# A hybrid encoder layer on one core: the order of feed-forward pairs, and buffers for copies of memory keys and values

## The chip, the core and the metric

The kernel runs on one core of one Trainium2 chip. A core has five engines that work side by side, each with a queue of its own that it serves in order: TensorE (matrix products; PE in the profile, and PEld for its weight loads), VectorE (DVE), ScalarE (ACT), GpSimd (POOL) and SyncE (SP), which here issues the DMA transfers between the device's memory (HBM) and the memory on the core (SBUF, 128 partitions wide). Products are gathered in PSUM, eight banks of 128 x 512 float32, which DVE and ACT read. The metric is the device time of one execution in microseconds (us), the median of several runs.

## The reference

One layer of an encoder for 1024 tokens of width 1024: a mixer (windowed attention beside a gated delta rule), a cross-attention into 256 memory tokens, and a feed-forward block, each between two RMS norms. What matters here is the memory's keys and values and the feed-forward block:

```python
def _memory_cross_attention(h, mem_n, w_q, w_kv, w_o):
    ...
    kv = mem_n @ w_kv
    k = kv[..., :D_MODEL].reshape(b, m, CROSS_HEADS, CROSS_HEAD_DIM).astype(jnp.float32)
    v = kv[..., D_MODEL:].reshape(b, m, CROSS_HEADS, CROSS_HEAD_DIM).astype(jnp.float32)
    ...

def _swiglu(h, w_gate_up, w_down):
    gu = h @ w_gate_up
    return (jax.nn.silu(gu[..., :D_FF]) * gu[..., D_FF:]) @ w_down
```

All inputs are float32; `D_FF` is 2816, and `w_gate_up` has 1024 rows and 2 x 2816 columns, the gate's columns first.

## The kernel before

Every large product is made of three: a float32 operand is split into a rounded part `hi` (a cast on ACT) and the rest `lo` (a subtraction on DVE, or on POOL where the code says so), and hi x hi, hi x lo and lo x hi are summed in PSUM. `load_w` and `pair_weights` load a raw weight block (`wraw`, two buffers in all) and split it.

The program is written with a framework that schedules: it takes the operations in the order of the code, with the priorities that the code sets for weight loads, models when each could run, and fixes from that one order for each engine. At run time each engine keeps to that order, and waits where an operand isn't ready. A buffer that is used again waits for the last readers of what it held, transfers out of it among them.

**Memory keys and values** (L883 to L912). They are computed while the mixer's scan runs, in slots of a hand-written order (`ORDER_3`): eight times `K`, keys for 128 columns, and then two times `V`, values for 512 columns and both halves of the memory tokens. Each result is copied by ACT from PSUM into a buffer (`cv`, 128 x 256, two buffers; `vv`, 128 x 512, one buffer) and stored to HBM from there. The last windows of the attention (`ptw`, `pow`, L598 to L666) are worked off among the `V`s, and behind them begins the output projection `mid_gemm` (`pmg`, L991), whose PSUM banks are those of the scan, the keys and the values.

**Feed forward, gate and up** (L1155 to L1306). The hidden width of 2816 is 22 blocks of 128 channels, taken in 11 pairs. For each pair, the gate's 256 columns and the up part's 256 columns are each one "weight" of 2 x 2 blocks, multiplied with the activations, 2 x 2 blocks as well, by Strassen's scheme in Winograd's form, with seven block products instead of eight. A block product (`product`, L1163) is 4 k-tiles x 3 parts = 12 matmuls of 128 x 512. In the code the products of one weight are

- A: the first block with X11, and later a second one with X21 added into the same bank;
- B: S2 with T2;
- D: S1 with T1, and later S4 with X22 added into the same bank;
- E: S3 with T3, and later W22 with T4 added into the same bank.

S1 to S4 are sums of weight blocks: POOL makes two of them from the raw blocks `a_` and `b_` (L1215, L1217) and DVE two (L1216, L1218); each is split (`s0h`/`s0l` to `s3h`/`s3l`: S1 is number 0, S2 number 1, S3 number 2, S4 number 3). W22, the lower half of `b_`, is split into `bhi` and `blo`. Between products DVE forms v = A + B (L1279) and u = v + D (L1281), and then the four quarters of the result (`quarter`): for the gate a sum on DVE and SiLU on ACT, for the up part a sum on DVE (`up`, L1242) and on POOL the product with the gate's quarter (L1243). v and u are read out of B's and D's banks before the second product into D may begin.

For the first EARLY = 4 pairs the two products into A are made before this loop, while the last activations are still being prepared (L1173 to L1190); they are kept in HBM (`d_m1`, and the finished quarter in `d_a["11"]`) and fetched in the loop (L1266, L1272). So an early pair has 10 products in the loop, a full one 14. A full pair also needs the whole first block `a_` split (`whi` on ACT, `wlo` on POOL, L1225); an early one doesn't.

For each pair the loop runs over its two weights twice: first A (if full), B, D, E of the gate and then of the up part, and then the second products. After the last quarter come four sums on DVE (`s1`, `s2`, `a21`, `s4`, L1297 to L1301); these and the quarters are stored to `d_a` for the down projection, by `put` behind the loads of the pair after (L1262). Down projection and final norm follow in `block_product` (L1334 to L1460). Index `kb` of the stores is the pair's number, so the order of the pairs makes no difference to what is computed.

Of the kernel before, what the change touches and what calls it, by code (L numbers as in the profile page):

```python
# [10 lines left out]
F32 = mybir.dt.float32  # L11
# [8 lines left out]
P = 128  # L20
# [9 lines left out]
ML = 256  # L30

EARLY = 4
# [43 lines left out]
def tile_hybrid_block(  # L76
# [31 lines left out]
    def pool(name, bufs, **kw):  # L108
        return tc.tile_pool(name=name, bufs=bufs, reuse_waits="tile", **kw)
# [8 lines left out]
    def load_w(src, k, n, eng=None, after=None):  # L118

        with tc.high_priority(AHEAD):  # L120
            raw = wp.tile([P, k, n], F32, tag="wraw", name="wraw")
            with ExitStack() as order_:
                if after:
                    order_.enter_context(tc.issue_after(after.ins))
                nc.sync.dma_start(raw, src.rearrange("(k p) n -> p k n", p=P))
            hi = wp.tile([P, k, n], F32R, tag="whi", name="whi")
            lo = wp.tile([P, k, n], F32R, tag="wlo", name="wlo")
            split(hi, lo, raw, eng=eng)
        return hi, lo
# [726 lines left out]
    mk = p2.enter_context(pool("mk", 1))  # L856
# [26 lines left out]
    def next_keys():  # L883

        ct = kv_done[0]
        kv_done[0] += 1
        whi, wlo = load_w(w_ckv[:, ct * P:(ct + 1) * P], KT, P, nc.gpsimd)
        pp = pc.tile([P, 512], F32, tag="pc", name="pck")[:, 0:ML]
        for k in range(KT):
            for i, (w, a) in enumerate(((whi, 0), (whi, 1), (wlo, 0))):  # L890
                nc.tensor.matmul(pp, w[:, k, :], mT[a][:, k, :], start=(k == 0 and i == 0), stop=(k == KT - 1 and i == 2))
        cv = mk.tile([P, ML], F32, tag="cv", name="cv", bufs=2)
        nc.scalar.copy(cv, pp)
        nc.sync.dma_start(d_mk[ct * P:(ct + 1) * P, :], cv)

    def next_values():

        ch = kv_done[1]
        kv_done[1] += 1
        pp = [pc.tile([P, 512], F32, tag="pc", name="pcv") for _ in range(2)]  # L900
        for kp in range(4):
            whi, wlo = load_w(w_ckv[kp * 256:(kp + 1) * 256, D + ch * 512:D + (ch + 1) * 512], 2, 512)
            for t in range(2):
                for kk in range(2):
                    k = 2 * kp + kk
                    for i, (w, a) in enumerate(((whi, 0), (whi, 1), (wlo, 0))):
                        nc.tensor.matmul(pp[t], mT[a][:, k, t * P:(t + 1) * P], w[:, kk, :], start=(k == 0 and i == 0),
                                         stop=(k == KT - 1 and i == 2))
        for t in range(2):
            vv = mk.tile([P, 512], F32, tag="vv", name="vv", bufs=1)  # L910
            nc.scalar.copy(vv, pp[t])
            nc.sync.dma_start(d_mv[t, :, ch * 512:(ch + 1) * 512], vv)  # L912

# [2 lines left out]
    def scan_step(pairs):  # L916

        for _ in range(4):
            for s_ in pairs:
                next(s_, None)  # L920

    issue(ORDER_3, {"s": lambda *gs: scan_step([scans[g] for g in gs]), "W": next_windows, "M": memory_norm,
                    "K": next_keys, "V": next_values})
    dump("d_pz", d_pz[0] + d_pz[1])
    dump("d_kv", d_kv)
# [230 lines left out]
    NF = FF // P  # L1156
    NB = NF // 2
# [5 lines left out]
    def product(out_, w, xx, start=True):  # L1163
        for k in range(HK):
            for i, (a, b_) in enumerate(((0, 0), (0, 1), (1, 0))):
                nc.tensor.matmul(out_, w[a][:, k, :], xx[b_][:, k, :], start=(start and k == 0 and i == 0),  # L1166
                                 stop=(k == HK - 1 and i == 2), skip_group_check=not start)
# [5 lines left out]
    for e in range(EARLY):  # L1173
        f = 2 * e
# [23 lines left out]
    def bank(name):  # L1198
        return pg.tile([P, 512], F32, tag="pg", name=name)
# [5 lines left out]
    def pair_weights(c0, early):  # L1205

        with tc.high_priority(AHEAD):
            raws = []
            for i in range(2):
                raws.append(wp.tile([P, KT, P], F32, tag="wraw", name="wraw"))  # L1210
                load = nc.sync.dma_start(raws[i], w_gate_up[:, c0 + i * P:c0 + (i + 1) * P].rearrange("(k p) n -> p k n", p=P))
            a_, b_ = raws
            s = [ws.tile([P, HK, P], F32, tag="sr", name="sr", bufs=3) for _ in range(4)]
            hl = {i: [ws.tile([P, HK, P], F32R, tag=f"s{i}{c}", name=f"s{i}{c}") for c in "hl"] for i in (1, 0, 2, 3)}
            nc.gpsimd.tensor_tensor(s[0], b_[:, 0:HK], b_[:, HK:], ALU.add)  # L1215
            nc.vector.tensor_tensor(s[1], s[0], a_[:, 0:HK], ALU.subtract)  # L1216
            nc.gpsimd.tensor_tensor(s[2], a_[:, 0:HK], b_[:, 0:HK], ALU.subtract)  # L1217
            nc.vector.tensor_tensor(s[3], a_[:, HK:], s[1], ALU.subtract)  # L1218
            for i in (1, 0, 2, 3):
                split(*hl[i], s[i])  # L1220
            W1 = None
            if not early:
                ahi = wp.tile([P, KT, P], F32R, tag="whi", name="whi")
                alo = wp.tile([P, KT, P], F32R, tag="wlo", name="wlo")
                split(ahi, alo, a_, eng=nc.gpsimd)  # L1225
                W1 = (ahi[:, 0:HK], alo[:, 0:HK]), (ahi[:, HK:], alo[:, HK:])
            W22 = [tg.tile([P, HK, P], F32R, tag=n, name=n) for n in ("bhi", "blo")]
            split(*W22, b_[:, HK:])
        return W1, W22, [hl[i] for i in range(4)], load
# [21 lines left out]
    def put(stores, after=None):  # L1251
        for dst, t in stores:
            with ExitStack() as order_:
                if after:
                    order_.enter_context(tc.issue_after(after.ins))
                nc.sync.dma_start(dst, t)

    for f in range(0, NF, 2):
        early = f // 2 < EARLY
        wts = [pair_weights(c0, early) for c0 in (f * P, FF + f * P)]  # L1260

        put(sums, wts[1][3])  # L1262
        act = {(r, hf): tg.tile([P, HALF], F32, tag=f"act{r}{hf}", name=f"act{r}{hf}", bufs=1)
               for r in range(2) for hf in range(2)}
        if early:
            nc.sync.dma_start(act[0, 0], d_a["11"][f // 2])  # L1266
        st = []
        for i, (W1, W22, (S1, S2, S3, S4), _) in enumerate(wts):
            a1, v, u = (tg.tile([P, 512], F32, tag=n, name=n, bufs=b_) for n, b_ in (("a1", 1), ("v", 2), ("u", 1)))
            A = None  # L1270
            if early:
                nc.sync.dma_start(a1, d_m1[f + i])  # L1272
            else:
                A = bank("pA")
                product(A, W1[0], X11)
                nc.scalar.copy(a1, A)
            B_, D_, E_ = (bank(n) for n in ("pB", "pD", "pE"))
            product(B_, S2, T2)
            nc.vector.tensor_tensor(v, a1, B_, ALU.add)  # L1279
            product(D_, S1, T1)  # L1280
            nc.vector.tensor_tensor(u, v, D_, ALU.add)  # L1281
            product(E_, S3, T3)
            quarter(i, act, 1, 1, u, E_)
            st.append((A, D_, E_, v))
        for i, (W1, W22, (S1, S2, S3, S4), _) in enumerate(wts):
            A, D_, E_, v = st[i]
            if A is not None:
                product(A, W1[1], X21, start=False)
                quarter(i, act, 0, 0, None, A)
            product(D_, S4, X22, start=False)  # L1290
            quarter(i, act, 0, 1, v, D_)
            product(E_, W22, T4, start=False)
            quarter(i, act, 1, 0, v, E_)
        kb = f // 2
        a11, a21, a12, a22 = (act[i] for i in ((0, 0), (0, 1), (1, 0), (1, 1)))
        s1, s2 = (tg.tile([P, HALF], F32, tag="sa", name="sa") for _ in range(2))
        nc.vector.tensor_tensor(s1, a21, a22, ALU.add)  # L1297
        nc.vector.tensor_tensor(s2, s1, a11, ALU.subtract)
        nc.vector.tensor_tensor(a21, a11, a21, ALU.subtract)
        s4 = tg.tile([P, HALF], F32, tag="up", name="s4")  # L1300
        nc.vector.tensor_tensor(s4, a12, s2, ALU.subtract)  # L1301
        nc.sync.dma_start(d_a["22"][kb], a22)
        if not early:
            nc.sync.dma_start(d_a["11"][kb], a11)
        sums = [(d_a[n][kb], t) for n, t in (("s1", s1), ("s2", s2), ("s3", a21), ("12", a12), ("s4", s4))]
# [187 lines left out]
```

## Time and profile before

| | us |
|---|---|
| median of 3 runs | 1600.72 (1600.3 to 1604.94) |
| profiled execution, its own time | 1601.45 |
| profiled execution, span from the first to the last instruction | 1599.7 |
| DVE busy over the span | 1034.0 |
| ACT busy over the span | 766.2 |
| POOL busy over the span | 522.8 |
| mean granted TensorE clock | 0.983 of full speed |

The profile is of one execution. Its rows name a line of the code (L1166), an engine, an operation, and the tiles written and read, with buffer numbers left out, and then shape and type; where a row gives a number in brackets, it is the idle time of that engine before the instruction, and what ended it. In the timeline a row begins with its start and length in us. A chain of waits is followed backwards from the last instruction: at each step to what released it. The granted clock is the share of full speed that the clock of TensorE had.

### The profile page before, as it was taken

How to read it: one execution, taken by the hardware profiler on the slowest of the kernel's cores; microseconds unless marked ns; L12 is line 12 of the kernel's file. 1: busy time of each engine (PE TensorE's matmuls, PEld its weight loads, DVE VectorE, ACT ScalarE, POOL GpSimd, SP SyncE). 2: the span in 40 equal slices, each digit the busy share in tenths (PEclk: the TensorE clock that was granted, in tenths of full speed). 3: DMA queues.
4: the chain of work that ended last, by engine and by line, in shares of the span. 5: the costliest groups of instructions: out<-in, count | busy, mean ns of one | idle time of the engine just before them, and what ended most of it. 6: DMA issues, size and time to landing. Idle time of an engine off the chain costs nothing. (4 is left out here: it accounts for less than half of the span.)

```text
span 1599.7 us, 21414 instructions
## 1 busy us (share of the span) xinstructions
PE 1523.6 (95%) x7558; PEld 1274.7 (80%) x7558; DVE 1034.0 (65%) x1596; ACT 766.2 (48%) x1561; POOL 522.8 (33%) x479
## 2 busy tenths in 40 slices
PE   6999889988899989999999999999999999999998
PEld 5877778877799967788888777778888888888786
DVE  6846886967677765454345549778765555587575
ACT  6566543326957785564334566223322323344532
POOL 2367653234335610243301140335433433100021
PEclk9999999998999999999999999999999999999999
DMA  6134258474999675354222254444333333763344
GB/s 205 41 109 124 59 159 239 129 192 122 296 324 277 193 266 191 145 185 152 73 69 80 90 185 139 150 157 152 100 120 118 104 99 99 272 222 108 110 169 160
DMA packets 265400, 247.29 MB, mean 155 GB/s; under 512 B 43960, under 2 KB 200525, under 8 KB 265293
## 3 DMA queue, kind: packets, MB, share of 16 engines
q1 hardware_dynamic: 265293, 245.93, 48.7%
q8 instruction: 59, 0.97, 0.3%
q14 instruction: 48, 0.39, 0.1%
HBM read 175.86 MB, written 67.40 MB: 152 GB/s over the span
## 5 line engine op out<-in xcount | busy, mean ns | idle before, releaser
L102 ACT CAST whi<-wraw 128x1024 fp32r<-128x1024 f32 x108 | 113.3, 1050 | 147.7 <-PE pA L1166 34.5
L103 POOL TENSOR_TENSOR wlo<-wraw,whi 128x1024 fp32r<-128x1024 f32 x48 | 118.4, 2467 | 165.2 <-ACT whi L102 150.8
L260 PE MATMUL pg<-hhi,whi 128*128 128x512 f32 x352 | 141.5, 403 | 0.0
L260 PE MATMUL pg<-hlo,whi 128*128 128x512 f32 x352 | 140.8, 401 | 0.0
L260 PE MATMUL pg<-hhi,wlo 128*128 128x512 f32 x352 | 140.8, 400 | 0.0
L103 DVE TENSOR_TENSOR wlo<-wraw,whi 128x1024 fp32r<-128x1024 f32 x60 | 75.5, 1260 | 86.0 <-ACT whi L102 76.5
L991 PE MATMUL pmg<-whi,b 128*128 128x512 f32 x384 | 120.0, 400 | 2.6 <-ACT whi L102 2.2
L1166 PE MATMUL pA<-s,whi 128*128 128x512 f32 x352 | 109.7, 393 | 1.4 <-ACT m L1183 1.4
L285 DVE SCALAR_TENSOR_TENSOR acc<-cp,cols,acc 128x1024 f32<-128x1024 f32 x48 | 77.8, 1622 | 34.8 <-ACT acc L283 34.1
L991 PEld LDWEIGHTS pmg<-whi,b 128*128 128x128 f32 x384 | 72.3, 191 | 18.2 <-ACT whi L102 2.7
L1243 POOL TENSOR_TENSOR act<-act,up 128x512 f32<-128x512 f32 x33 | 48.2, 1460 | 103.9 <-DVE up L1242 46.1
L260 PEld LDWEIGHTS pg<-hhi,wlo 128*128 128x128 f32 x352 | 67.5, 192 | 13.3
L260 PEld LDWEIGHTS pg<-hhi,whi 128*128 128x128 f32 x352 | 67.6, 192 | 13.2 <-ACT hhi L102 0.3
L260 PEld LDWEIGHTS pg<-hlo,whi 128*128 128x128 f32 x352 | 67.4, 191 | 13.1
L1354 PE MATMUL pdX<-dhl,whi 128*128 128x512 f32 x264 | 76.1, 391 | 1.5 <-DVE zv L1409 0.8
L1166 PEld LDWEIGHTS pA<-s,whi 128*128 128x128 f32 x352 | 65.3, 188 | 15.2 <-ACT m L1183 2.0
L1384 POOL TENSOR_SCALAR frs<-sq 128x1 f32<-128x1 f32 x8 | 11.9, 1497 | 195.8 <-ACT jk L1373 194.9
L1215 POOL TENSOR_TENSOR sr<-wraw 128x512 f32<-128x512 f32 x22 | 29.0, 1318 | 134.1 <-DMA wraw<-in_w_gate_up_dram 120.9
L991 PE MATMUL pmg<-wlo,b 128*128 128x512 f32 x192 | 71.5, 392 | 0.0
L1166 PE MATMUL pA<-s,wlo 128*128 128x512 f32 x176 | 68.8, 392 | 1.6 <-DVE wlo L103 1.6
L102 ACT CAST whi<-araw 128x1024 fp32r<-128x1024 f32 (+1 forms) x36 | 35.4, 982 | 71.3 <-PE pdX L1354 27.6
L103 DVE TENSOR_TENSOR wlo<-araw,whi 128x1024 fp32r<-128x1024 f32 (+1 forms) x36 | 40.8, 1133 | 39.6 <-ACT whi L102 39.4
(411 smaller groups left out, 4272.5 us busy)
## 6 DMA issues: line engine op xcount, KB each, us to landing
wraw<-in_w_gate_up_dram SPq DMA_DIRECT2D x52, 512.0 KB, 4.1
kv<-d_kv SPq DMA_DIRECT2D x32, 512.0 KB, 6.9
wraw<-in_w_in_dram SPq DMA_DIRECT2D x22, 512.0 KB, 4.0
b<-in_w_down_dram SPq DMA_DIRECT2D x20, 512.0 KB, 5.9
araw<-d_as SPq DMA_DIRECT2D x20, 512.0 KB, 3.8
d_kv<-kv SPq DMA_DIRECT2D x8, 1024.0 KB, 6.3
pz<-d_pz SPq DMA_DIRECT2D x32, 256.0 KB, 6.6
wraw<-in_w_ckv_dram SPq DMA_DIRECT2D x16, 512.0 KB, 6.4
```

The lines of the kernel that those rows point to most:

```text
L102: nc.scalar.copy(hi, src)
L103: (eng or nc.vector).tensor_tensor(lo, src, f32(hi), ALU.subtract)
L260: nc.tensor.matmul(p_, w[:, k, :], ah[a][:, k, :], start=(k == 0 and i == 0), stop=(k == nk - 1 and i == 2))
L285: nc.vector.scalar_tensor_tensor(acc, cp[:, t:t + S], taps[t], acc, ALU.mult, ALU.add)
L991: nc.tensor.matmul(pp[t], act[a][:, k, tt], w_[:, kk, :], start=(k == 0 and i == 0), stop=(k == KT - 1 and i == 2))
L1166: nc.tensor.matmul(out_, w[a][:, k, :], xx[b_][:, k, :], start=(start and k == 0 and i == 0), stop=(k == HK - 1 and i == 2), skip_group_ch ...
L1215: nc.gpsimd.tensor_tensor(s[0], b_[:, 0:HK], b_[:, HK:], ALU.add)
L1243: nc.gpsimd.tensor_tensor(o_, o_, up, ALU.mult)
L1354: nc.tensor.matmul(banks[t], a[:, k - k0, tt], w, start=(first and k == 0 and i == 0), stop=(k == NB - 1 and i == 2), skip_group_check=not ...
L1384: nc.gpsimd.tensor_scalar(rs, sq[:, 1, t:t + 1], sq[:, 0, t:t + 1], D * EPS, ALU.add, ALU.add)
```

## The change

There are two edits.

The loop over the pairs no longer takes them from 0 to 10, but an early one (with its first products at hand) and a full one in turn, and then the rest: 0, 4, 1, 5, 2, 6, 3, 7, 8, 9, 10. Each pair does what it did before.

The copies of the memory's keys and values use one tag, `cv`, with two buffers of 512 columns, in place of two buffers of 256 columns for the keys and one of 512 for the values. The keys use the first 256 columns of theirs.

```diff
@@ next_keys
-        cv = mk.tile([P, ML], F32, tag="cv", name="cv", bufs=2)
+        cv = mk.tile([P, 512], F32, tag="cv", name="cv", bufs=2)[:, 0:ML]
         nc.scalar.copy(cv, pp)
         nc.sync.dma_start(d_mk[ct * P:(ct + 1) * P, :], cv)
@@ next_values
         for t in range(2):
-            vv = mk.tile([P, 512], F32, tag="vv", name="vv", bufs=1)
+            vv = mk.tile([P, 512], F32, tag="cv", name="vv", bufs=2)
             nc.scalar.copy(vv, pp[t])
             nc.sync.dma_start(d_mv[t, :, ch * 512:(ch + 1) * 512], vv)
@@ tile_hybrid_block
-    for f in range(0, NF, 2):
+
+    turns = [p for e in range(EARLY) for p in (e, EARLY + e)] + list(range(2 * EARLY, NB))
+    for f in (2 * p for p in turns):
         early = f // 2 < EARLY
         wts = [pair_weights(c0, early) for c0 in (f * P, FF + f * P)]
```

Since the framework fixes the order of each engine from a model of the whole, other instructions move with them. On TensorE the built order differs from that before in two places: among the last attention windows, the values and the first products of the output projection, and in the loop over the pairs. Up to the first and between the two it is the same.

## The prediction

> **What bounds the kernel now.** I read the page first, then the work of each engine by stage, then the chain of waits, and last the timeline of TensorE where the stage rows show idle time.
>
> ```profile
> span 1599.7 us, 21414 instructions
> ...
> PE 1523.6 (95%) x7558; PEld 1274.7 (80%) x7558; DVE 1034.0 (65%) x1596; ACT 766.2 (48%) x1561; POOL 522.8 (33%) x479
> ...
> PE 33%; DMA 1%; DVE 1%; ACT 0%; POOL 0%; issue 0%; SPq 0%; DVEq 0%; POOLq 0%; ACTq 0%
> ```
>
> TensorE is busy for 95% of the span and carries the chain; no other engine is near. So a change can win only in TensorE's idle time or in matmuls that run slowly. The profiled execution took 1601.45 us, 1.75 more than its span, and lies 0.73 above the median of the runs (1600.72); the sums below are made against 1601.45. Both edits sit in stretches that these rows divide (busy time of PE, PEld, DVE, ACT and POOL in each, then the granted clock, the DMA share and GB/s):
>
> ```profile
> 996.07:1379.78 383.71, 378.94 (x1658) 311.76 (x1658) 248.06 (x319) 115.77 (x183) 138.39 (x88) 1.00 0.39 126
> 996.07:1105.00 108.93, 104.16 (x446) 84.17 (x446) 82.81 (x105) 30.97 (x51) 38.84 (x26) 0.98 0.48 152
> 1105.00:1379.78 274.78, 274.78 (x1214) 227.59 (x1213) 165.25 (x215) 84.80 (x132) 99.55 (x62) 1.00 0.35 116
> ```
>
> The first row is the whole loop over pairs, from the first product of pair 0 to the last of pair 10. It has 4 early pairs of 10 products and 7 full pairs of 14: 138 products. One product of 12 matmuls takes 2.72 us in the chain below, so the loop could take 138 x 2.72 = 375.4 us; it takes 383.7. The 8.3 us between are all before 1105: from there TensorE is busy for the whole 274.78 us. Of the 8.3, the idle time is 383.71 - 378.94 = 4.8. The chain of waits (start, length, what) shows the largest piece:
>
> ```profile
> 1039.98 4.87 DMA wraw<-in_w_gate_up_dram
> ...
> 1045.04 1.26 POOL sr L1215
> ...
> 1046.33 1.76 DVE sr L1216
> ...
> 1049.42 0.60 DVE s1l L103
> ...
> 1050.62 0.61 DVE u L1281
> ...
> 1051.36 4.36 PE pD L1166 x12
> 1055.73 2.97 PE pE L1166 x12
> 1058.69 2.72 PE pB L1166 x12
> ```
>
> Read backwards: the second product into pD of pair 1's up weight could not start before `u` was read out of that bank (L1281). On DVE `u` stood behind the preparation of the next weight (pair 2's gate), whose sums waited for POOL's, and these for a load issued at 1039.98. TensorE's timeline has this wait and the other three (idle time in brackets):
>
> ```profile
> 997.82 0.51 PE L1166 MATMUL pB<-b,s1l 128*128 128x512 f32 x1 [1.02 <-DVE s1l L103]
> ...
> 1006.32 0.70 PE L1166 MATMUL pD<-x,s3h 128*128 128x512 f32 x2 [0.46 <-DVE u L1281]
> ...
> 1020.38 0.74 PE L1166 MATMUL pB<-b,s1h 128*128 128x512 f32 x2 [0.21 <-ACT s1h L102]
> ...
> 1029.60 0.39 PE L1166 MATMUL pE<-b,blo 128*128 128x512 f32 x1
> ...
> 1047.96 0.39 PE L1166 MATMUL pE<-b,blo 128*128 128x512 f32 x1
> 1051.36 0.70 PE L1166 MATMUL pD<-x,s3h 128*128 128x512 f32 x2 [3.02 <-DVE u L1281]
> ```
>
> 1.02 + 0.46 + 0.21 + 3.02 = 4.7 us, which is the idle time. After the last one the product at 1051.36 takes 4.36 instead of 2.72 and the next 2.97: 1.64 + 0.25 = 1.9 us more.
>
> Why was the load so late? It needed the buffer of the weight before it, and so the last read of that, `blo` on DVE:
>
> ```profile
> 1035.53 0.69 DVE L1297 TENSOR_TENSOR sa<-act,act 128x512 f32<-128x512 f32 x1 [1.18 <-POOL act L1243]
> ...
> 1039.04 0.68 DVE L103 TENSOR_TENSOR blo<-wraw,bhi 128x512 fp32r<-128x512 f32 x1
> ```
> ```profile
> 1031.99 0.62 ACT L102 CAST bhi<-wraw 128x512 fp32r<-128x512 f32 x1
> ```
>
> Its cast was done on ACT at 1032.6, but `blo` came at 1039.04, since DVE met it behind the sums of pair 0 (L1297 and on), which wait for POOL's products of gate and up, and these for the end of pair 0 on TensorE.
>
> **The feed-forward edit.** It removes and adds no instruction: the pairs run as 0, 4, 1, 5, 2, 6, 3, 7, 8, 9, 10. Loads, splits and stores come in the same number, and SP has the same transfers in another order. What moves is which pair follows which, and with it how much TensorE work covers the chain just read. Call U the end of pair 0's last product on TensorE, 1029.60 + 0.23 = 1029.8. `blo` starts 9.2 after U, the load is issued 10.2 after it, and `u` is done (1050.62 + 0.61) at U + 21.4. Before, TensorE has between U and that `u` 21 matmuls and five products: 4.8 + 13.6 = 18.4. That is 3.0 short, the stall.
>
> In the changed kernel's built order, DVE meets the same things in the same sequence: sums of pair 0, `blo`, preparation of the next pair's gate (now pair 1 behind pair 4), then `u`. TensorE now has 28 matmuls of pair 4's gate (6.3), four products of its up weight (10.9), the three second products of the gate (8.2) and one of the up weight (2.7): 28.1. The chain of 21.4 ends 6.7 us before it is asked for. So 3.02 goes, and with it I take the 1.9 of slow matmuls behind it. Gain: 4.9.
>
> The clock rule has to be weighed here. The page "TensorE: Matmul & The Clock Gate" of the Trainium skill (Part 1: The HAM clock gate) puts the fall to half speed after an idle window of about 3.4 us, and the return after about as much work. The idle time here was 3.02 and half speed followed, so the trace is a little under the rule. If by that rule the slow matmuls were not this stall's, 1.9 less would be gained and the time be about 1596.7.
>
> What full pairs bring with them: per weight a cast on ACT and one split on POOL, and the product A must wait for both. POOL's split is long:
>
> ```profile
> L103 POOL TENSOR_TENSOR wlo<-wraw,whi x8: 2392/2400/2649, 1096.4 to 1223.0; 128x1024 fp32r<-128x1024 f32 x8
> ...
> DMA to landing us min/median/max: 3.6/4.1/6.5
> ```
> ```profile
> 1009.42 0.38 SPq L1211 DMA_DIRECT2D wraw<-in_w_gate_up_dram  x1
> ```
>
> It now stands on POOL ahead of the sums for pair 4's gate, in the tightest place of the loop, where the third weight was already 0.21 late (1020.38). The raw block for it is issued at 1009.42; with 4.1 to land, about 1.1 for the cast and 2.4 for the split it is done at 1017.0, and A can start at 1020.2. The sums are at most 2.4 later than before, and A itself gives them 2.72 of cover. So no stall is added and the 0.21 goes; without that cover it would be 2.4 - 0.2 = 2.2 more. If the load takes its longest 6.5, the split ends at 1019.4: still in time. The first two waits, 1.02 and 0.46, stay, since pair 0 is prepared as before.
>
> Then the meeting of a full pair with the early one behind it. Call V the moment at which the second products of pair 4 begin. In the built order `blo` of pair 1's gate stands on DVE behind the reads of the gate's D and E, which come at V + 8.2; with two reads of 0.6 it starts at V + 9.4. From the issue of a load to the end of `s1l` the chain above took 1049.42 + 0.60 - 1039.98 = 10.0, so pair 1's up weight is ready at V + 19.4. TensorE asks for it after the six second products (16.3) and three first ones of pair 1's gate (8.2), at V + 24.5: 5.1 to spare. This meeting comes three times, after pairs 4, 5 and 6; I take nothing for it, and rival 2 has its price. SP serves its queue in order, and pair 1's second load of `a1` now stands behind the stores of pair 4's sums, some 6 us after V + 16.3 as after U above (1035.53 - 1029.8); what is computed from it must be ready only at the second product into that D, at V + 16.3 + 16.3 + 5.4 = V + 38, so 10 us and more are left. Pairs 7 to 10 run as they do now, without a stall.
>
> Sum for the edit: -3.02 - 1.9 - 0.21 = -5.1.
>
> **The copies of keys and values.** Storage is equal: two buffers of 256 columns and one of 512 before, two of 512 after. The eight copies of keys and four of values, and their stores, stay. What comes is that the first value copies use buffers of the last keys, whose copy ends at 564.9 + 0.4, 18 us before the first value is copied (583.7, the row below it): nothing. What goes is the rule that a value's copy needs the store of the one before it landed:
>
> ```profile
> L893 ACT COPY cv<-pck x8: 350/364/375, 439.8 to 564.9; 128x256 f32<-128x256 f32 x8
> ```
> ```profile
> L911 ACT COPY vv<-pcv x4: 583/590/596, 583.7 to 607.4; 128x512 f32<-128x512 f32 x4
> ...
> DMA to landing us min/median/max: 2.3/2.5/2.8
> ```
> ```profile
> 603.67 0.59 ACT L911 COPY vv<-pcv 128x512 f32<-128x512 f32 x1 [0.55 <-PE pcv L907]
> ...
> 606.87 0.58 ACT L102 CAST ph<-ptw 128x512 fp32r<-128x512 f32 x1
> 607.35 0.60 ACT L911 COPY vv<-pcv 128x512 f32<-128x512 f32 x1
> ```
> ```profile
> 605.82 0.50 PE L661 MATMUL pow<-ph,vhi 128*128 128x512 f32 x1 [0.40 <-ACT ao L665]
> ...
> 607.51 0.50 PE L661 MATMUL pow<-ph,vhi 128*128 128x512 f32 x1 [0.72 <-ACT ph L102]
> 607.84 0.63 PE L991 MATMUL pmg<-whi,s 128*128 128x512 f32 x2
> ...
> 631.74 0.73 PE L991 MATMUL pmg<-whi,s 128*128 128x512 f32 x2 [1.49 <-DVE z L995]
> ```
>
> The last copy was placed at 607.35, 3.1 us behind the end of the third. In the built order the copies now stand in twos, the last ahead of `ao`, so the banks of the output projection (pmg, L991) come free earlier and TensorE gets 20 of its matmuls (4.5 us) before the two reads of attention weights that waited 0.40 and 0.72. I take these 1.1 as gained. The bounds: nothing, if a bank or the weights for pmg come late, or if the 1.49 at 631.74 (it hangs on loads and splits, not on TensorE) grows by what was won; and a loss of one DVE split, 1.26, since splits of the mixer's output now stand ahead of `pl` (L103) there:
>
> ```profile
> L103 DVE TENSOR_TENSOR wlo<-wraw,whi 128x1024 fp32r<-128x1024 f32 x60 | 75.5, 1260 | 86.0 <-ACT whi L102 76.5
> ```
>
> The other wait of the neighbourhood, for weights at 589.06, has its loads in the same place, and so stays with the slow matmuls behind it:
>
> ```profile
> 586.69 0.50 PE L661 MATMUL pow<-ph,vhi 128*128 128x512 f32 x1 [0.90 <-ACT ph L102]
> ...
> 589.06 2.08 PE L907 MATMUL pcv<-whi,mT 128*128 128x512 f32 x4 [1.58 <-ACT whi L102]
> ```
> ```profile
> 590.00:600.00 10.00, 10.00 (x40) 8.20 (x39) 3.79 (x9) 8.29 (x21) 0.93 (x2) 0.74 0.74 246
> ```
>
> 0.90 + 1.58 us are idle, and 0.26 of the 10 us after them, 2.6, is lost to the clock. With the same idle time I leave both; if the slow matmuls did not follow, it would be 2.6 less.
>
> Together: 1601.45 - 5.1 - 1.1 = 1595.2 for a profiled execution, 1594.5 on the scale of the median. I forecast 1594.8.
>
> **Rivals.** (1) The feed-forward gain comes, the one of the copies doesn't (for the reason of the 1.49): 1601.45 - 5.1 = 1596.3, or 1595.6 to 1596.3. The row at 631.74 speaks for it; against it, the loads of the mixer's output are no later in the built order. (2) Slower: the meeting full to early. If the chain from `blo` to `s1l` is longer than its 5.1 of cover, TensorE stalls three times, and each stall of about 3 us drags 1.9 of slow matmuls: 3 x 4.9 - 6.2 = +8.5, so 1610. It decides from a chain of over 15.1 us instead of 10.0; two loads at their longest (6.5 against 4.1) add 2.4, POOL's split ahead of a sum another 2.4, which makes 14.8. That is close below, which keeps it alive. (3) The change does nothing that shows: the order moves the 3 us stall to another place in the loop, as the start of pair 4 (2.2 plus 1.9 slow) would; 1601.45 - 6.2 + 4.1 = 1599.3.
>
> Beside (3) stands a rule that speaks against the edit: "GPSIMD Engine Reference" of the Trainium skill (section 1, Specifications) says that POOL shares its way to SBUF with VectorE when that reads two SBUF inputs. The 1.76 of the DVE sum at 1046.33, beside 0.60 for its neighbours, agrees. By it each of the six splits of pairs 4 to 6 slows a DVE operation by up to 1.76 - 0.60 = 1.2 us; each place has 2.7 to 6.7 of cover, so the sum stays.
>
> **Numbers.** Forecast 0.50; (1) 0.17; (2) 0.14; (3) 0.19. The measurement can tell about 0.3%, 4.8 us: faster is below 1595.9, slower above 1605.5. The forecast lies 1.1 below that border, so I give 0.45 of its 0.50 to faster, and of (1), which straddles it, 0.08: faster 0.53, slower 0.14, and the same for the rest, 0.33. Range: below, 1594.5 - 2.6 - 1.5 (the wait at 631.74 gone) = 1590.4; above, (2) with one stall in three places is 1594.8 + 4.9 = 1599.7 and with two 1604.6. So 1590 to 1604, which leaves out most of (2).
>
> **What would show it.** Right: in the profile after, the loop's idle time is near 1.5 us, all before 1007; the second products of each up weight follow without a wait on `u`; TensorE's clock is full from 1000 to the end of the loop, and the loop takes about 378.6. The row of pmg starts near 605 and the waits 0.40 and 0.72 are gone. Wrong: a wait on `s1l`, `s1h` or `u` at the first product of an early pair's up weight (rival 2), on `wlo` at a pA (rival 3), or a longer wait on `z` at the second column half of pmg (rival 1). A time over 1600 would mean that the cover argument is false.

## The result and the profile after

The changed kernel took 1591.57 us (median of 7 runs, 1588.77 to 1597.28), the kernel before 1600.72 (7 runs, 1599.53 to 1604.94). The ratio is 0.9958, with a 95% interval of 0.9942 to 0.9974: 4 to 9 us less, 6.7 in the middle. (The two medians are 9.2 apart, at the upper end of that interval.) The forecast was 1594.8, 5.9 less. The execution that was profiled is the slowest of the seven, at 1597.28. So the trace shows where time went, and not how much the median gained.

The page and the stage rows of the kernel after, the same views as before. The three stage rows are the loop over pairs from the first pB to the end, and its two parts (PE, PEld, DVE, ACT and POOL busy, granted clock, DMA share, GB/s):

```profile
span 1595.6 us, 21420 instructions
...
PE 1518.7 (95%) x7558; PEld 1270.4 (80%) x7558; DVE 1047.7 (66%) x1596; ACT 764.3 (48%) x1561; POOL 525.2 (33%) x479
...
PE 37%; DVE 1%; ACT 1%; DMA 1%; issue 0%; SPq 0%; POOL 0%; DVEq 0%; POOLq 0%; ACTq 0%
```
```profile
997.89:1375.80 377.91, 376.30 (x1656) 310.60 (x1657) 260.09 (x319) 114.12 (x183) 141.96 (x88) 1.00 0.40 128
997.89:1105.00 107.11, 105.50 (x462) 86.34 (x463) 82.90 (x99) 33.23 (x54) 44.19 (x27) 1.00 0.44 138
1105.00:1375.80 270.80, 270.80 (x1196) 224.26 (x1195) 177.18 (x221) 80.89 (x129) 97.77 (x61) 1.00 0.38 125
```

The loop takes 377.9 where it took 383.7, and its idle time is 377.91 - 376.30 = 1.6 instead of 4.8. All of it lies before 1105, and in that part the clock is 1.00 where it was 0.98. The timeline of TensorE has the waits that are left, and the product that had waited 3.02: the second product into pD of the up weight, now of pair 4, starts at 1060.32 with no bracket behind it.

```profile
999.65 0.50 PE L1166 MATMUL pB<-b,s1l 128*128 128x512 f32 x1 [1.02 <-DVE s1l L103]
...
1008.24 0.70 PE L1166 MATMUL pD<-x,s3h 128*128 128x512 f32 x2 [0.58 <-DVE u L1283]
```
```profile
1060.32 0.61 PE L1166 MATMUL pD<-x,s3h 128*128 128x512 f32 x2
```

The chain of the prediction is still there, and no shorter. DVE's and SP's timelines of the kernel after:

```profile
1042.14 0.68 DVE L103 TENSOR_TENSOR blo<-wraw,bhi 128x512 fp32r<-128x512 f32 x1
...
1049.00 1.76 DVE L1216 TENSOR_TENSOR sr<-sr,wraw 128x512 f32<-128x512 f32 x1 [3.61 <-POOL sr L1215]
...
1054.00 0.69 DVE L1283 TENSOR_TENSOR u<-v,pD 128x512 f32<-128x512 f32 x1
```
```profile
1042.61 0.43 SPq L1256 DMA_DIRECT2D d_a<-act  x1
1043.13 0.40 SPq L1211 DMA_DIRECT2D wraw<-in_w_gate_up_dram  x1
```

U, the moment at which TensorE has issued pair 0's last product and takes up the next, is 1032.2 here. `blo` ends at U+10.6, the load is issued at U+10.9 and `u` is read at U+22.5 (1054.00 + 0.69). Before it was U+21.4. TensorE asks for it at U+28.1.

The other edit sits some 400 us earlier. TensorE, ACT and DVE of the kernel after:

```profile
592.75 1.20 PE L907 MATMUL pcv<-whi,mT 128*128 128x512 f32 x4 [1.39 <-ACT whi L102]
...
606.48 0.71 PE L991 MATMUL pmg<-whi,s 128*128 128x512 f32 x2
...
631.79 0.78 PE L991 MATMUL pmg<-whi,s 128*128 128x512 f32 x2 [1.93 <-DVE z L995]
```
```profile
604.95 0.59 ACT L911 COPY vv<-pcv 128x512 f32<-128x512 f32 x1 [0.63 <-PE pcv L907]
605.87 0.59 ACT L911 COPY vv<-pcv 128x512 f32<-128x512 f32 x1 [0.33 <-PE pcv L907]
606.35 0.36 ACT L664 COPY ao<-pow 64x256 f32<-64x256 f32 x1
```
```profile
628.59 2.55 DVE L103 TENSOR_TENSOR b<-b,b 128x1024 fp32r<-128x1024 f32 x2 [0.42 <-ACT b L102]
631.05 1.88 DVE L995 TENSOR_TENSOR z<-pmg,gpost 128x512 f32<-128x512 f32 x3
```

The two last copies stand together, ahead of `ao`, and the output projection (pmg) starts at 606.48, with neither the 0.40 nor the 0.72 ahead of it. But at its second column half it now waits 1.93 for `z`, where it waited 1.49.

Where the 4.2 us between the ends of the two traces come from (us; the memory stretch runs from the first pcv to the last first-half product of pmg, that is until TensorE turns from blocks named s to blocks named b):

| stretch | before | after | difference |
|---|---|---|---|
| start to the first pcv | 567.1 | 570.7 | +3.6 |
| memory stretch (copies) | 86.3 | 84.4 | -1.9 |
| to the first early product | 290.6 | 290.7 | +0.1 |
| early products | 52.1 | 52.1 | 0 |
| loop over pairs | 383.5 | 377.9 | -5.6 |
| rest, to the last product | 212.2 | 211.8 | -0.4 |

The first row has nothing to do with the change: up to there both kernels issue the same work in the same order, and in the traces of the twelve kernels compared below it ran from 563.4 to 570.7. So one trace's end can't be compared with another's to better than a few us. Only stretches can, and medians of many runs.

### The profile page after: what moved, and what is told of

Read it like the earlier page. It is cut to its first block, busy times and chain, and to the rows that moved or that the text cites. A ratio compares the mean times of both kernels' runs of the same rounds, so it can differ in the third digit from the quotient of the medians.

```text
span 1595.6 us, 21420 instructions
## 1 busy us (share of the span) xinstructions
PE 1518.7 (95%) x7558; PEld 1270.4 (80%) x7558; DVE 1047.7 (66%) x1596; ACT 764.3 (48%) x1561; POOL 525.2 (33%) x479
## 5 line engine op out<-in xcount | busy, mean ns | idle before, releaser
L103 DVE TENSOR_TENSOR wlo<-araw,whi 128x1024 fp32r<-128x1024 f32 (+1 forms) x36 | 40.8, 1132 | 38.7 <-ACT whi L102 38.6
```

The costliest lines, as they stand in the source:

```text
L103: (eng or nc.vector).tensor_tensor(lo, src, f32(hi), ALU.subtract)
```

## The experiments

In each diff the minus line is the kernel before. "Loop" is the time from the first pB to the first product of the down projection; it was 383.5 before and is 377.9 after by that measure.

**Both edits again, each alone.** `e0_both` is the changed kernel, run once more beside the parts.

> The changed kernel once more, beside its two halves on the same chip. Theory (two separate gains: about 5 to 6 us from the order of the pairs, which gives TensorE cover for a late weight, and 1 to 2 us from the copies): 6 to 8 us under the kernel before; the loop over the pairs, from the first product of the first pair to the first product into pdA, takes about 378 us instead of 383.7. Rival (the order of the pairs is worth its 5 us and the rest of the measured gain was chance): about 5 us under.

```diff
-    for f in range(0, NF, 2):
+    turns = [p for e in range(EARLY) for p in (e, EARLY + e)] + list(range(2 * EARLY, NB))
+    for f in (2 * p for p in turns):
```

> The order of the pairs alone; keys and values have their buffers of before. Theory: the loop takes about 378 us, as with both edits, and the time is 5 to 6 us under the kernel before. Rival (the copies' edit shifts the loop's weight loads and so helps the loop): the loop stays over 380 us.

```diff
-        cv = mk.tile([P, ML], F32, tag="cv", name="cv", bufs=2)
+        cv = mk.tile([P, 512], F32, tag="cv", name="cv", bufs=2)[:, 0:ML]
...
-            vv = mk.tile([P, 512], F32, tag="vv", name="vv", bufs=1)
+            vv = mk.tile([P, 512], F32, tag="cv", name="vv", bufs=2)
```

> The shared buffers alone; the pairs run 0 to 10. Theory: from the first matmul of the values (pcv) to the last product of the output projection's first half (pmg with s) the stretch is 1 to 2 us shorter, 1 to 2 us in all, and the loop keeps its 383.7 with the 3 us wait on u. Rival (the waits on ao and ph are only passed on to z at the second half of the columns): 0 us, with a wait on z longer by what was won.

The third way to the copies leaves the keys in 256 columns and gives the values a second buffer of their own:

```diff
-        cv = mk.tile([P, ML], F32, tag="cv", name="cv", bufs=2)
+        cv = mk.tile([P, ML], F32, tag="cv", name="cv", bufs=1)
...
-            vv = mk.tile([P, 512], F32, tag="vv", name="vv", bufs=1)
+            vv = mk.tile([P, 512], F32, tag="vv", name="vv", bufs=2)
```

> The kernel before, with two buffers of 512 columns for the values under their own tag and one buffer of 256 for the keys: no sharing, but the second buffer that the values' copies lacked. Theory (what helps is that a value's copy no longer waits for the store of the one before): the same as the shared buffers alone, 1 to 2 us under the kernel before, with the copies in twos. Rival (it is the sharing, or the places that other work got with it): no gain, or a loss from keys that now wait for their own stores.

Against the same 27 runs of the kernel before (median 1599.13):

| kernel | median, us | runs | ratio | 95% interval | loop |
|---|---|---|---|---|---|
| both | 1592.84 | 10 | 0.9951 | 0.9933 to 0.9969 | 377.6 |
| order only | 1589.85 | 6 | 0.9939 | 0.9915 to 0.9962 | 377.5 |
| shared buffers only | 1598.93 | 12 | 0.9987 | 0.9972 to 1.0003 | 383.8 |
| two buffers for values | 1598.77 | 12 | 0.9999 | 0.9981 to 1.0017 | 384.8 |

The order of the pairs makes the whole gain that can be told. Its interval is a gain of 6.1 to 13.6 us, above the 5 to 6 expected, while the loop in its trace is only 6.0 shorter; what the median gained beyond the loop no stretch of the trace explains. With the copies alone, the wait on `u` stands where it stood, and slow matmuls follow it:

```profile
1048.86 1.19 PE L1166 MATMUL pD<-x,s3h 128*128 128x512 f32 x2 [2.91 <-DVE u L1281]
```

In all four kernels with copies in twos the 0.40 and 0.72 are gone, but on average the stretch is no shorter. One wait behind them shows why. The first column half of pmg ends, and the second can begin only when `z` (L995) has read a bank; on DVE `z` stands behind the splits of the mixer's output (`b`), and these wait for their loads. TensorE's row at that point, with the order alone, with the copies alone, and with both:

```profile
630.38 0.74 PE L991 MATMUL pmg<-whi,s 128*128 128x512 f32 x2 [1.24 <-DVE z L995]
```
```profile
628.70 1.22 PE L991 MATMUL pmg<-whi,s 128*128 128x512 f32 x2 [2.79 <-DVE z L995]
```
```profile
631.04 1.22 PE L991 MATMUL pmg<-whi,s 128*128 128x512 f32 x2 [4.20 <-DVE z L995]
```

1.24 without the copies, 2.79 and 4.20 with them. ACT's timeline of the last of the three, with the casts of `b` whose split DVE does ahead of `z`:

```profile
626.29 1.05 ACT L102 CAST b<-b 128x1024 fp32r<-128x1024 f32 x1 [1.02 <-DMA b<-d_mix]
628.08 1.04 ACT L102 CAST b<-b 128x1024 fp32r<-128x1024 f32 x1 [0.74 <-DMA b<-d_mix]
```

Each waits for its load. Counted from the first pcv, the four traces with copies in twos (after, both again, and the two with copies alone) start pmg at 35.6 to 36.8, the other eight at 38.5 to 40.8: some 3.8 earlier. But `z` starts at 61.4 on average (60.3 to 62.9) against 62.6 (61.8 to 63.9), only 1.2 earlier. The rest of what was moved ahead turns into the longer wait. And in these traces half speed follows that wait where it is 1.93 or more: from the start of `z` to the end of the stretch it then takes 23.9 to 24.6, in three of the four with copies in twos and in one of the eight, and else 22.4 to 22.5. So on average nothing is left. The whole stretch takes 83.5 to 87.5 in the four, 85.2 on average, and 84.2 to 86.5 in the eight, 85.2 on average. The shortest of all twelve is the one of the four that kept full speed (two buffers for values, 83.5), so the loss at `z` hangs on the clock, and that isn't settled by the length of the wait (see the last section).

**One full pair, and where it has to stand.** The prediction reckoned with cover at each meeting of two pairs. If that is all, each meeting of early pairs needs its own full pair between them; if lateness exists only at the loop's start, one full pair is enough, but has to come there.

```diff
-    for f in range(0, NF, 2):
+    turns = [0, 4, 1, 2, 3] + list(range(5, NB))
+    for f in (2 * p for p in turns):
```

> Order 0, 4, 1, 2, 3, 5 to 10, buffers of before: one full pair behind pair 0, then three early ones in a row. Theory A (as forecast: an early pair directly behind an early one has 18.4 us of TensorE work against a chain of 21.4): the wait on u comes back once, now at pair 1 with pair 2 behind it, about 3 us and 1.9 of slow matmuls; the loop takes 382 to 384 us. Theory B (the preparation of weights is only late at the start of the loop; a lead won once is kept): one full pair is enough, no wait, and the loop takes about 378 us.

`e4_late_full` has turns = [0, 1, 4, 2, 5, 3] and then 6 to 10:

> Order 0, 1, 4, 2, 5, 3, 6 to 10, buffers of before: the two first early pairs stay together, and full ones come in turn after them. Theories A and B: pair 1's up weight meets the late preparation of what follows, pair 4's gate, as it met pair 2's: a wait on u of about 3 us (more if the split on POOL is in front, up to 5.4) with slow matmuls after it, the loop at 382 to 386 us. Rival (what the change won comes from spreading early pairs over the whole loop, with their fetches and stores): three of four early pairs are still apart, so the loop is near 379 us.

`e6_early_last` has turns 4 to 10, then 0 to 3:

> Order 4 to 10 and then 0 to 3, buffers of before: all early pairs in a row, at the end of the loop. Theory A: a wait on u or s1 at the meetings 0 to 1, 1 to 2 or 2 to 3, 3 us each with slow matmuls behind it; the loop at 382 us or over. Theory B: the lead is there by then, no wait at the end; at the start the product A covers pair 4's sums, so the loop takes 376 to 379 us.

| order of the pairs | median, us | ratio | 95% interval | loop |
|---|---|---|---|---|
| 0, 4, 1, 2, 3, 5 to 10 | 1593.46 | 0.9958 | 0.9941 to 0.9974 | 377.5 |
| 0, 1, 4, 2, 5, 3, 6 to 10 | 1597.67 | 0.9994 | 0.9977 to 1.0010 | 386.2 |
| 4 to 10, 0 to 3 | 1600.36 | 1.0001 | 0.9980 to 1.0023 | see below |

(10 runs each, against 31 of the kernel before, median 1598.47.) One full pair behind pair 0 brings all of it, as far as these intervals can tell. Its waits on TensorE from 985, some 13 us ahead of the loop, to the loop's end (total us, times, longest):

```profile
PE pB L1166 <- DVE s1l L103: 1.0, 1, 1.0
PE pA L1166 <- ACT m L1183: 0.7, 1, 0.7
PE pD L1166 <- DVE u L1283: 0.3, 1, 0.3
```

Pairs 1, 2 and 3 follow each other there as before, and nothing waits. So Theory A fails: an early pair behind an early one doesn't always have only 18.4 us of cover against a chain of 21.4. The spread order that leaves 1 behind 0 keeps the stall, and adds one ahead of it:

```profile
1039.98 0.73 PE L1166 MATMUL pD<-x,s3h 128*128 128x512 f32 x2 [1.29 <-DVE u L1283]
...
1048.55 1.19 PE L1166 MATMUL pD<-x,s3h 128*128 128x512 f32 x2 [2.84 <-DVE u L1283]
```

With all full pairs first, the early pairs at the end of the loop don't stall at all. TensorE is busy for all of the time from 1060 to the loop's end (the row's columns as above):

```profile
1060.00:1374.30 314.30, 314.30 (x1389) 260.24 (x1388) 202.94 (x263) 95.30 (x150) 111.57 (x72) 1.00 0.41 134
```

But the start costs more than it did, and this I had not priced. The second weight of a loop that starts with a full pair waits for its sums:

```profile
1009.75 1.22 PE L1166 MATMUL pB<-b,s1h 128*128 128x512 f32 x2 [5.87 <-ACT s1h L102]
```

From the first early product to the end of the loop it takes 436.6, where before took 435.6 and after 430.0. Its fourth raw block was issued at 1001.84, right behind the end of a `blo` that ran from 999.35 to 1001.81, and that `blo` waited for a cast which stood behind the wide one of pA's weight. The expectation of 376 to 379 for the loop fails on this start, not on the end.

**What holds the load.** The prediction named `blo` on DVE as the cause of the late load. So `blo` of the early pairs goes to POOL:

```diff
-            split(*W22, b_[:, HK:])
+            split(*W22, b_[:, HK:], eng=nc.gpsimd if early else None)
```

> Order 0 to 10 and buffers of before; in early pairs the split blo of the lower half of b is made by POOL and not by DVE. If the late release of b by blo, which stands on DVE behind the sums of the pair before, is what makes the load late, then the load behind pair 1's up weight is issued several us earlier than 10.2 us after the end of pair 0, the wait on u falls from 3 to under 1 us, and the loop takes about 379 us. If the chain is late for another reason (POOL's products, DVE's order), the wait stays at about 3 us and the loop at 382 us or over.

This kernel, `e10_blo_pool`: 1597.21 (10 runs), ratio 0.9988 (0.9967 to 1.0008), loop 384.4. The wait on `u` shrinks only from 3.02 to 2.02, and the third weight of the loop is now 1.30 late. POOL's, SP's and TensorE's timelines:

```profile
1034.16 1.29 POOL L103 TENSOR_TENSOR blo<-wraw,bhi 128x512 fp32r<-128x512 f32 x1
```
```profile
1036.03 0.34 SPq L1256 DMA_DIRECT2D d_as<-sa  x1
1036.46 0.39 SPq L1211 DMA_DIRECT2D wraw<-in_w_gate_up_dram  x1
```
```profile
1047.90 0.70 PE L1166 MATMUL pD<-x,s3h 128*128 128x512 f32 x2 [2.02 <-DVE u L1281]
```

`blo` is done at 1035.46, but the load is issued at 1036.46, 1.0 later: in SP's queue a store of a pair's sums (L1256) stands ahead of it, and SP serves its queue in order. In the kernel before, the last store ahead of the load was issued at 1039.56 and `blo` ended at 1039.72, so both were in the way, and the trace of before could not tell them apart. Two kernels do: the stores go to ACT's queue, without and with `blo` on POOL.

```diff
-                nc.sync.dma_start(dst, t)
+                nc.scalar.dma_start(dst, t)
```

> The order and the buffers of before; only the stores of a pair's sums are issued from ACT's queue instead of SP's. Called U, as in the prediction, the end of pair 0's last product on TensorE: before, the load that the 3.02 wait hangs on was issued at U+10.2 (1039.98), 0.26 after `blo` had ended on DVE (1039.04 + 0.68) and 0.42 after the last store ahead of it in SP's queue (1039.56). Theory Q (both hold the load, the later one decides, and they end together): with the stores gone from SP the load still waits for `blo`, so it is issued at U+9.5 to U+10.2, the wait on `u` stays at 2.5 to 3.1 and the loop at 383 to 384.5; ratio 0.998 to 1.001. Rival D (SP's queue alone held it): load near U+8, wait 0.5 to 1.5, loop near 381.

> As e10_blo_pool (early pairs' `blo` on POOL), and the stores of the sums from ACT's queue. In e10_blo_pool `blo` ended on POOL at U+8.3 (1034.16 + 1.30, U = 1027.14) but the load was issued only at U+9.3 (1036.46), right behind a store of the sums at 1036.03 in SP's queue; `u` was done at U+20.6 and TensorE waited 2.02. Theory Q: with both out of the way the load is issued at U+8.3 to U+8.8, `u` is done at U+19.6 to U+20.1, the wait on `u` shrinks to 1.0 to 1.6, and the loop to 381.5 to 383.5 if the start of the loop is as in e10_blo_pool. Rival L (the load does not set `u`; the order of POOL and DVE behind it does): `u` stays at U+20.4 or later and the wait at 1.8 or more, although the load comes earlier.

| kernel | median, us | ratio | 95% interval | loop |
|---|---|---|---|---|
| stores on ACT's queue (`e12_actq`) | 1600.29 | 1.0008 | 0.9992 to 1.0023 | 388.4 |
| the same, `blo` on POOL (`e11_pool_actq`) | 1594.75 | 0.9970 | 0.9946 to 0.9994 | 382.7 |

(10 runs each, against 19 of the kernel before, median 1600.29.) Stores alone: DVE's `blo`, the load on SP, POOL's sum that waits for it, and TensorE's wait:

```profile
1033.62 0.68 DVE L103 TENSOR_TENSOR blo<-wraw,bhi 128x512 fp32r<-128x512 f32 x1
```
```profile
1034.32 0.38 SPq L1211 DMA_DIRECT2D wraw<-in_w_gate_up_dram  x1
```
```profile
1040.71 1.28 POOL L1215 TENSOR_TENSOR sr<-wraw 128x512 f32<-128x512 f32 x1 [7.57 <-DMA wraw<-in_w_gate_up_dram]
```
```profile
1047.06 0.70 PE L1166 MATMUL pD<-x,s3h 128*128 128x512 f32 x2 [4.18 <-DVE u L1281]
```

The load goes the moment `blo` ends (1034.30), only 0.2 earlier after U than before, as the theory that both hold it says. The wait and the loop, 4.18 and 388.4, lie outside that theory's 2.5 to 3.1 and 383 to 384.5. That the wait is 4.18 and not 3.0 is the load itself, which POOL had 6.4 after its issue (1034.32 to 1040.71); in the other kernels of the table below that took 3.8 to 5.0. TensorE waits for `u` four times in this loop, 7.7 in all; ahead of the wait of 2.34 at 1106.66, too, a load was slow (7.0 from its issue to POOL's sum). With both out of the way:

```profile
1033.55 0.37 SPq L1211 DMA_DIRECT2D wraw<-in_w_gate_up_dram  x1
```
```profile
1044.81 0.70 PE L1166 MATMUL pD<-x,s3h 128*128 128x512 f32 x2 [0.85 <-DVE u L1281]
...
1073.80 0.70 PE L1166 MATMUL pD<-x,s3h 128*128 128x512 f32 x2 [1.54 <-DVE u L1281]
```

The load goes at U+8.2, as `blo` ends, and the wait is 0.85, a little less than the 1.0 to 1.6 expected. But pair 2 now waits 1.54 for its `u`, which did not wait before, so the loop is only 0.8 shorter than before. Its load was issued at 1058.92, and POOL's sum could begin only at 1066.95, 8.0 later; before, the same took 5.4. And with `blo` on POOL the third weight of the loop is 1.28 late here, as it was 1.30 late in `e10_blo_pool`, where before it was 0.21. (The median fell by more, 0.9946 to 0.9994 as a ratio; what lies beyond the 0.8 no stretch of the trace explains.) The chain in all kernels (us from U; the column of work is when TensorE had nothing left but the product that waits for `u`, or asked for it):

| kernel | U | `blo` done | load issued | POOL has it | `u` done | work ends | wait |
|---|---|---|---|---|---|---|---|
| before | 1029.8 | 9.9 | 10.2 | 15.2 | 21.4 | 18.5 | 3.02 |
| after | 1032.2 | 10.6 | 10.9 | 15.5 | 22.5 | 28.1 | none |
| e4_late_full | 1025.6 | 12.0 | 12.1 | 15.8 | 22.8 | 20.1 | 2.84 |
| e10_blo_pool | 1027.1 | 8.3 | 9.3 | 13.6 | 20.6 | 18.8 | 2.02 |
| e11_pool_actq | 1025.4 | 8.2 | 8.2 | 12.5 | 19.3 | 18.6 | 0.85 |
| e12_actq | 1024.4 | 9.9 | 10.0 | 16.4 | 22.6 | 18.5 | 4.18 |

In every row with a wait it is the end of `u` less the end of the work, within 0.25. The chain is the right one, over a range of 3.5 us, and the only kernels with real room are those that give TensorE ten more us of work.

Of the versions tried, the order alone has the lowest median, 1589.85. Its interval overlaps with that of both edits, so that it is the better one isn't shown. A second pair of buffers for the raw blocks, which by this account would take the rule behind this chain away, wasn't tried.

## Why the prediction was right, and where it was not

**The stall on `u` (-3.02) and the slow matmuls behind it (-1.9): right.** Both are gone (the clock is full through the whole loop), and the loop lost 5.6 to 6.0 us (after, both again, order only) where 5.1 was forecast. The working left 1.6 of its 8.3 without a term (8.3 - 4.8 - 1.9); in the kernel after that rest is 0.9 (377.9 - 375.4 - 1.6), which is most of the difference. The chain was given 21.4 and is 22.5, TensorE's work 28.1 and is 28.1, so the spare time was 5.6 instead of 6.7. The copies alone and the late full pair keep stall and slow matmuls together.

**Why it was late only there.** The prediction gave the cover before as 18.4 and did not ask why pairs 2 and 3, which also follow early ones, don't stall. The rows of the kernel before answer it (TensorE and DVE, first for pair 0, then for pair 2):

```profile
1020.38 0.74 PE L1166 MATMUL pB<-b,s1h 128*128 128x512 f32 x2 [0.21 <-ACT s1h L102]
...
1024.28 0.70 PE L1166 MATMUL pD<-x,s3h 128*128 128x512 f32 x2
```
```profile
1023.51 0.69 DVE L1281 TENSOR_TENSOR u<-v,pD 128x512 f32<-128x512 f32 x1
```
```profile
1080.34 0.70 PE L1166 MATMUL pD<-x,s3h 128*128 128x512 f32 x2
```
```profile
1079.51 0.68 DVE L1281 TENSOR_TENSOR u<-v,pD 128x512 f32<-128x512 f32 x1
```

Pair 0's own up weight was late: its `u` was read at 1024.20 and its second product began at 1024.28. TensorE had not stood still before that, because the order puts 15 matmuls of pair 1's gate there (1020.38 to 1024.28). These 15, 3.4 us, are then missing as cover one pair later. Pair 2 has all of its own, 18.4 + 3.4 = 21.8, and its `u` is done at 1080.19 for a product that begins at 1080.34. So early pairs in a row just keep up. The lateness made at the loop's start was covered there by work pulled ahead, and it becomes a stall at the next place, where that work is missing. No run takes only these 15 matmuls away; that the lateness begins at the loop's start and not at each meeting is what the runs show. One full pair, with four more products for TensorE, makes up for it. That is what the order 0, 4, 1, 2, 3 shows, and the four early pairs without a wait at the end of `e6_early_last`.

**The 0.21 at the third weight: right, and the cover that carried it too.** POOL's split for pair 4 ran from 1017.05 to 1019.46 in the kernel after, pA followed at 1021.94 without a wait. The 1.02 stayed (1.02); the 0.46 became 0.58.

**Full pair before early pair, three times, at nothing: right.** V, where the second products of pair 4 begin, is 1049.44. The load was forecast for V+9.4 and came at V+9.7 (1059.12; the working left out the 0.7 that `blo` itself takes, but had its start 0.4 too late); `s1l` for V+19.4 and ended at V+19.8; TensorE asked at V+24.5, as forecast. Rival 2, three new stalls and 1610, and rival 3, a stall elsewhere, have no row in the trace. The splits of the full pairs did cost DVE time: its 319 instructions of the loop were busy for 260.09 us instead of 248.06. If the six splits of pairs 4 to 6 made all of these 12.0, that is an estimated 2.0 each, more than the 1.2 that the prediction set as the most; the cover held it, and TensorE had no wait from it.

**The cause of the late load: half of it.** "`blo` came at 1039.04, since DVE met it behind the sums" is true, but `blo` off DVE brings 1.0 of the 3.0 only, as SP's queue held the load as well. For the change itself this cost nothing, since it leaves both where they are.

**The copies (-1.1): this step failed, and rival 1 holds.** The two waits went, as said, and counted from the first pcv pmg started at 35.7 instead of 40.7. The step that failed is taking the 1.1 as gained when the next wait, 24 us on, hangs on loads. The prediction named this as the bound "nothing", and that was the value to take. Rival 1 had all of the gain eaten by the wait; in the traces about 1.2 does arrive at `z`, and goes back behind it to the clock, as in three of the four the longer wait is followed by half speed. With the copies alone the ratio's interval of 0.9972 to 1.0003 runs from a gain of 4.5 us to a loss of 0.5, and the stretch's average is the same with and without. A small gain isn't excluded by that; it isn't shown.

**The wait on weights at 589.06 "stays", with its slow matmuls: not so steady.** In the kernel after it is 1.39 at 592.75, and from 590 to 600 the clock was full, where before it was 0.74. That is part of the -1.9 in the table of stretches. I don't count it as a gain of the change: at the next such wait, on `z`, the clock fell instead, to 0.74 from 630 to 635.

So the sum came out near the middle of the interval with two terms off by about one us each in opposite directions: the loop brought 0.5 to 0.9 more than forecast, the copies about 1.1 less. That the sum fits so well is luck in this part; that the stall goes, and why, is not.

## What to carry to other kernels

A chain that runs against TensorE is priced by two numbers at each place where it comes round, the length of the chain and the work that TensorE has left, and the second must leave out whatever was already pulled ahead to fill an earlier wait. Where steps of different length are to be had, the long one belongs where the lateness is made, and one may be enough. Filling a wait by starting the next stage earlier was worth nothing that could be told here: the next wait there hangs on loads, and it grew. And a load can be held by its buffer and by its queue at once: moving one of the two shows the other.

## What the hardware did that I had not expected

Half speed came after much shorter idle time than I had thought possible. In the loop, a second product into pD took 3.0 after waits of 0.85, 1.29 and 1.54, and 4.2 to 5.5 after 2.02, 2.84, 2.91, 3.02 and 3.10; after 4.18 it took 4.6. At `z`, waits of 1.15 to 1.65 left the clock full, and 1.93, 2.26, 2.79 and 4.20 were followed by matmuls at 0.43 instead of 0.23 each. The page "TensorE: Matmul & The Clock Gate" of the Trainium skill (Part 1: The HAM clock gate) has the clock fall after an idle window of about 3.4 us; these rows, with half speed behind 1.93 and 2.02, don't agree with that.

But no border can be read from these two places, since the length of the wait alone doesn't decide. In the loop of `e12_actq` a second product into pD took 3.0 after a wait of 2.34. Some 35 us behind `z`, the output projection waits for a weight, 2.23 or 2.24 us in all twelve traces; half speed follows in nine of them and not in three. And a wait of 3.27 to 3.32, which all twelve have between 185 and 189, is followed by half speed in seven and not in five. The rows of the kernel before, of `e6_early_last` and of `e12_actq` (five matmuls in 2.50 us at half speed, eight in 2.11 at full):

```profile
666.90 2.50 PE L991 MATMUL pmg<-whi,b 128*128 128x512 f32 x5 [2.23 <-ACT whi L102]
```
```profile
662.12 2.11 PE L991 MATMUL pmg<-whi,b 128*128 128x512 f32 x8 [2.23 <-ACT whi L102]
```
```profile
1106.66 0.70 PE L1166 MATMUL pD<-x,s3h 128*128 128x512 f32 x2 [2.34 <-DVE u L1281]
```

What else decides, these runs don't show. So the slow matmuls behind a stall of two or three us are a likely cost here, and not a sure one. Where several waits come close together, as ahead of 590, shorter ones can do it. This is the stretch from 590 to 595 in the kernel before, with the order alone, and in the kernel after (the granted clock is the third number from the end):

```profile
590.00:595.00 5.00, 5.00 (x16) 4.15 (x15) 2.06 (x5) 3.32 (x7) 0.93 (x2) 0.50 0.94 321
```
```profile
590.00:595.00 5.00, 5.00 (x20) 4.17 (x20) 2.91 (x6) 3.99 (x9) 0.93 (x2) 0.66 0.97 326
```
```profile
590.00:595.00 5.00, 3.26 (x16) 2.42 (x17) 4.96 (x10) 2.40 (x5) 0.06 (x1) 1.00 1.03 364
```

It is 0.50 behind waits of 0.90 and 1.58, 0.66 behind 0.92 and 1.56, and 1.00 in the kernel after, which has waits of 0.29 and 1.39 there. But behind 0.30 and 1.73 with both edits again it was 1.00 too, and behind 0.29 and 1.32 with two buffers for values 0.84. The plainest pair is 0.90 and 1.66 in `e10_blo_pool`, which left the clock full, and 0.93 and 1.66 in `e6_early_last`, which were followed by half speed. So what decides there stays open as well.

The other surprise is how much the same work scatters. The first pcv, ahead of which TensorE's order is the same in eleven of the twelve traces (with two buffers for values it differs), starts between 563.4 and 570.7, and the load of the table took 3.8 to 6.4 us from its issue to POOL in the same place of the loop.
